# Small products of a mixer set back behind their feeders, and an MLP's turns with another share for GpSimd

## The chip, the cores and the metric

The kernel runs on one core of a Trainium2 chip. The metric is the device time of one execution in microseconds (us), the median over runs. A core has TensorE (PE: matrix products, with a separate weight load, PEld), VectorE (DVE), ScalarE (ACT), GpSimd (POOL) and SyncE (SP, which here issues all DMA transfers). Every engine works through its own instructions in order; they wait for each other through semaphores.

## The reference

Two layers of an encoder on 1024 tokens of 1024 features, all in float32:

```python
for l in range(DEPTH):
    h = rms_norm(x, norm_mix[l])
    z = h @ w_in[l]                       # 2560 columns: q k v | q_h i_h f_fw f_bw g_h | a_c g_c
    o_att = block_attention(q_a, k_a, v_a)            # 8 heads of 64, 2 kv heads, QK norm, axial RoPE
    o_hg  = hgrn2_bidirectional(q_h, i_h, f_fw, f_bw, g_h, ...)   # 4 heads, gated recurrence both ways
    o_cv  = conformer_conv(a_c, g_c, ...)             # gate, depthwise conv of 31 taps, LayerNorm, swish
    x = x + concat([o_att, o_hg, o_cv]) @ w_out[l]
    h = rms_norm(x, norm_mlp[l])
    x = x + jnp.square(jax.nn.relu(h @ w1[l])) @ w2[l]      # 1024 -> 4096 -> 1024
```

## The kernel before

Activations lie with features on the 128 partitions and tokens along the free axis, in tiles of 128 x 1024. A float32 product is made of three passes over parts of reduced precision: `split` (L203) and `parts` (L894) copy a value to a high part on ScalarE and subtract it on VectorE for the low part; then high x high, high x low, low x high go to TensorE. A dense column (`zsteps`, L300, through `dense_steps`, L214) is 48 products of 128 x 512 into one of the two S banks of PSUM; its weights are split by `wtile` (L194), its result is taken out by `evac` (L316, L322) times the norm's factor.

**The mixer.** Twenty columns of z come in the order `ZORDER`: the convolution's four, then those of the first `Hgrn` object (two of the four recurrence heads), v, k, four of q, then those of the second. The convolution is 62 shifted multiply-adds on VectorE (L344, L352) and a LayerNorm (`conv_tail`). The recurrence (`Hgrn.core`) starts with `near`, goes through levels of block length 1 to 64, each with score products (`scores`, L494, taken out by VectorE at L501 or by predicated copies at L505) and updates (L525 on VectorE and GpSimd, L526), then transposes its keys (L539), makes the states (L549, L555, L558) and the outputs (L583, taken out at L587). The parts for v, k and q (`vpart`, `kpart`, `qpart`) square, sum over tokens (`tok_sums`, L162), take a root in a chain of some 11 small VectorE instructions (`rstd`, L151 to L156), rotate (`rope`, L621 to L624) and store. A row of factors is widened by ScalarE (`widen`, L168) and transposed by TensorE (`flip`, L178).

These parts are Python generators. A `yield` marks where another part may put its instructions; `next` on a generator emits them up to the next `yield`. So the place of a `yield` sets which instructions stand between a feeder and its consumer. Before the attention this loop mixes three of them: the q, k and v columns (`qg`), the convolution (`cg`) and the first recurrence:

```python
for _ in h0.core():
    for g in (qg, cg, qg, cg):
        next(g, None)
```

The framework then orders each engine's instructions by priority (the order in which they were written, or higher under `tc.high_priority`) and by when it takes their inputs to be ready. The result is the order shown below.

**Attention** runs 64 units (a head, a half, 128 queries): scores two units ahead (L745), VectorE's scaling with the row's extreme (L756), exponent (ScalarE, L759), division (GpSimd, L761), transposes (L782), values (L803). `gen`, the second recurrence, is taken one step at every second unit. Where it ends, the output projection's inputs for the recurrence and the convolution are split.

**The MLP** uses a seven-product scheme (M1 to M7, as Strassen's and Winograd's) on blocks, once for each of its two matrices. The first matrix goes in 16 pairs of tiles; `product` makes 12 products for one M and takes out the bank (ScalarE at L1022 to L1039; VectorE in `join`, L1004, then the activation at L1008 and L1009, and differences at L1035 and L1042 to L1044). Four M ahead, `w_parts` and `x_parts` make sums and differences (L904, L907) and splits. For the first 14 products (two pairs, taken side by side) the splits follow each other in written order (`ordered`). `row[0]` is the engine of the sums; it becomes GpSimd at product 10, and VectorE again 14 before the end. The results go to DRAM (`ad`) and come back as operands of the second matrix (`load_a`, L1063), into tiles m (14 buffers) or xs. The second matrix goes in 28 turns; `collect` adds banks to the residual (`acc`, L1175), which `load_acc` (L1098) brings from DRAM: four tiles of kind x, four of kind m.

## Time and profile before

| | us |
|---|---|
| median of three runs | 2546.32 |
| lowest, highest | 2542.85, 2547.26 |
| the profiled execution, its span | 2548.54, 2546.8 |
| busy in the span: PE, DVE, ACT, POOL | 2451.1, 2003.2, 1202.9, 779.0 |
| mean granted TensorE clock | 0.988 of full |

A page of the profile gives one execution: busy time by engine, the chain of work that ended last, the groups of instructions by source line. Views of the trace give the same for a window of time. "a<-b" is what an instruction writes and reads, "[2.21 <-DVE tmp L1004]" the idle time of its engine before it and what ended it. Line numbers are those of the kernel before.

### The profile page before, as it was taken

The page shows a single profiled execution, that of the slowest core. Times are in us where ns is not written, and L with a number is a line of the kernel's source. Part 1 is how long each engine was busy: PE and PEld are TensorE (multiplying, and loading weights), DVE is VectorE, ACT ScalarE, POOL GpSimd, SP SyncE. Part 2 cuts the span into 40 slices and gives each one's busy share as a digit, 9 for nine tenths or more (in the row PEclk, how much of TensorE's full clock was granted, in tenths as well). Part 3 has the DMA queues.
Part 4 walks back from the last instruction along what each step waited for, and adds up shares of the span by engine and source line. Part 5 has one row for each costly group of instructions (what it writes and reads, how often), then busy time and mean ns, then how long its engine had stood idle before and what let it go on. Part 6 is the DMA issues. An engine that isn't in the chain of part 4 may idle for free.

```text
span 2546.8 us, 34055 instructions
## 1 busy us (share of the span) xinstructions
PE 2451.1 (96%) x12608; PEld 2020.0 (79%) x12608; DVE 2003.2 (79%) x3023; ACT 1202.9 (47%) x1960; POOL 779.0 (31%) x491
## 2 busy tenths in 40 slices
PE   8989999999999999999999899999999999999999
PEld 7767778878778887888887777888787888878887
DVE  5998598872887777987859985898639877789876
ACT  4222478863544443443423225787635444444332
POOL 0232566433154430000123325664331544200000
PEclk9999999999999999999999999999999999999999
DMA  4101310032244448454221113000322444574442
GB/s 157 60 25 63 103 35 18 14 124 96 83 168 158 148 166 302 162 175 152 69 106 50 42 63 104 18 18 26 133 90 95 163 143 167 191 260 155 162 155 91
DMA packets 113077, 286.99 MB, mean 113 GB/s; under 512 B 11408, under 2 KB 11664, under 8 KB 112912
## 3 DMA queue, kind: packets, MB, share of 16 engines
q1 hardware_dynamic: 112912, 284.83, 32.2%
q8 instruction: 99, 1.62, 0.3%
q14 instruction: 66, 0.54, 0.1%
HBM read 197.75 MB, written 87.03 MB: 112 GB/s over the span
## 4 chain that ended last, share of the span: by engine, by line
PE 77%; DVE 14%; ACT 3%; issue 2%; POOL 2%; DMA 1%; SPq 0%; DVEq 0%; ACTq 0%; POOLq 0%
PE S L223 15%; PE S L1195 10%; PE c L995 9%; PE e L1195 7%; PE c L1195 6%; PE e L995 6%; PE S L995 6%; DVE x L352 4%; PE e L803 4%; PE c L782 3%; PE S L745 3%; PE e L494 2%; PE e L162 1%; PE e L583 1%; DVE P L756 1%
## 5 line engine op out<-in xcount | busy, mean ns | idle before, releaser
L223 PE MATMUL S<-xs,whi 128*128 128x512 f32 x1280 | 363.7, 405 | 10.4 <-ACT xs L208 8.9
L223 PEld LDWEIGHTS S<-xs,whi 128*128 128x128 f32 x1280 | 243.3, 193 | 66.2 <-ACT xs L208 8.9
L223 PE MATMUL S<-xs,wlo 128*128 128x512 f32 x640 | 203.3, 398 | 0.0
L1195 PE MATMUL S<-xs,xs 128*128 128x512 f32 x816 | 201.2, 390 | 0.3 <-DVE xs L897 0.3
L896 ACT ACTIVATE xs<-m 128x512 fp32r<-128x512 f32 x216 | 126.0, 619 | 157.4 <-DVE m L907 52.3
L761 POOL TENSOR_SCALAR P<-P,mx 128x1024 f32<-128x1024 f32 x124 | 142.4, 1149 | 162.8 <-DVE mx L760 125.3
L787 DVE TENSOR_TENSOR PT<-c,PT 128x512 fp32r<-128x512 f32 x256 | 171.1, 684 | 23.0 <-ACT PT L786 21.5
L786 ACT ACTIVATE PT<-c 128x512 fp32r<-128x512 f32 x256 | 147.3, 593 | 67.7 <-PE c L782 64.2
L1195 PEld LDWEIGHTS S<-xs,xs 128*128 128x128 f32 x816 | 153.1, 188 | 32.8 <-DVE xs L897 1.2
L199 ACT ACTIVATE whi<-raw 128x1024 fp32r<-128x1024 f32 x56 | 59.1, 1058 | 245.9 <-PE S L223 232.8
L803 PE MATMUL e<-PT,x 128*128 128x256 f32 x1024 | 172.3, 298 | 0.8 <-ACT PT L786 0.5
L756 DVE TENSOR_SCALAR_CACHE_REDUCE P<-S,nqc 128x1024 f32<-128x1024 f32 x124 | 158.6, 1279 | 13.9 <-PE S L745 8.7
L352 DVE SCALAR_TENSOR_TENSOR x<-x,par,x 128x1009 f32<-128x1009 f32 (+14 forms) x120 | 166.7, 1390 | 1.8
L897 DVE TENSOR_TENSOR xs<-m,xs 128x512 fp32r<-128x512 f32 x216 | 144.9, 694 | 24.8 <-ACT xs L896 24.8
L260 POOL TENSOR_TENSOR tmp<-tmp,tmp 128x1024 f32<-128x1024 f32 x19 | 50.6, 2664 | 364.4 <-ACT tmp L259 364.2
L782 PE MATMUL c<-cons,P 128*128 128x128 f32 x992 | 151.9, 277 | 10.5 <-POOL P L761 5.6
L745 PE MATMUL S<-x,QS 128*128 128x512 f32 x480 | 153.8, 419 | 4.9 <-DVE P L756 4.6
L759 ACT ACTIVATE P<-P,mx 128x1024 f32<-128x1024 f32 x124 | 142.5, 1149 | 24.6 <-DVE P L756 23.3
L1195 PE MATMUL e<-xs,xs 128*128 128x512 f32 x552 | 142.9, 395 | 7.2 <-ACT xs L896 6.8
L803 PEld LDWEIGHTS e<-PT,x 128*128 128x128 f32 x1024 | 138.9, 193 | 8.5 <-ACT PT L786 2.2
L782 PEld LDWEIGHTS c<-cons,P 128*128 128x128 f32 x992 | 115.1, 141 | 36.7 <-issue 10.4
L223 PEld LDWEIGHTS S<-xs,wlo 128*128 128x128 f32 x640 | 122.4, 192 | 26.6 <-issue 0.3
(310 smaller groups left out, 5679.3 us busy)
## 6 DMA issues: line engine op xcount, KB each, us to landing
m<-ad SPq DMA_DIRECT2D x104, 512.0 KB, 3.8
ad<-x SPq DMA_DIRECT2D x176, 256.0 KB, 2.1
raw<-w_in_t SPq DMA_DIRECT2D x40, 512.0 KB, 3.3
xs<-w_t SPq DMA_DIRECT2D x36, 512.0 KB, 3.8
raw<-w_t SPq DMA_DIRECT2D x36, 512.0 KB, 3.6
m<-w_t SPq DMA_DIRECT2D x32, 512.0 KB, 6.3
ad<-tmp SPq DMA_DIRECT2D x48, 256.0 KB, 2.2
x<-w_t SPq DMA_DIRECT2D x24, 512.0 KB, 4.8
```

The costliest lines, as they stand in the source:

```text
L223: nc.tensor.matmul(zp[h] if type(zp) is list else zp[:, h, :], w, xx[:, h * 512 : (h + 1) * 512], start=first, stop=last)
L352: nc.vector.scalar_tensor_tensor(y[:, lo:hi], u[:, lo + d : hi + d], par[:, l, wof + tap : wof + tap + 1], y[:, lo:hi], op0=ALU.mult, op1= ...
L745: nc.tensor.matmul(S[:, hb, :], qs, kk[:, hb * 512 : (hb + 1) * 512], start=first, stop=not first)
L756: nc.vector.tensor_scalar(Pt, S, nqc[:, j, ci : ci + 1], 3.0e38, op0=ALU.mult, op1=ALU.min, accum_out=mx[:, 1:2])
L759: nc.scalar.activation(Pt, Pt, AF.Exp, bias=mx[:, 1:2], scale=-1.0, accum_out=mx[:, 2:3])
L782: nc.tensor.transpose(t[:, q * P : (q + 1) * P], Pt[:, hb, q * P : (q + 1) * P], ident)
L786: nc.scalar.activation(hi, src, AF.Copy)
L787: nc.vector.tensor_tensor(lo, src, hi.bitcast(F32), op=ALU.subtract)
L803: nc.tensor.matmul(pvp[:, cs], VS[g][:, hb * 4 + kb, :], pt[:, kb, :], start=hb == 0 and n == 0, stop=hb == 1 and n == 7,)
L897: ordered("v", nc.vector.tensor_tensor(lo, src, hi.bitcast(F32), op=ALU.subtract))
L995: nc.tensor.matmul(bank, w[i][:, kt * P : (kt + 1) * P], BC[name][kt][j], start=n == 0 and name not in ("M6", "M7", "M3"), stop=n == 11, s ...
L1195: nc.tensor.matmul(banks[dt], w[i][:, dt * P : (dt + 1) * P], a[j], start=n == 0 and name not in ("M6", "M7", "M3"), stop=n == 3 * SG - 1, ...
```

## The change

In the mixer:

- `conv_tail` pauses four and six times between widening and transposing.
- The transposes of the recurrence's v (L442) leave the constructor of `Hgrn` and become `turned`, called from `near` behind two pauses, with one more after each half.
- The key transposes (L539) pause after every half instead of every two.
- `kpart` pauses twice more. The unfinished parts of q, k and v are resumed one step at a time (`resume`), at other steps of the next column, instead of being finished in one go.
- In attention, `gen` takes a step at every unit below 14, then at every second.

In the MLP:

- The bank reads and what follows them in `product` run under high priority for pairs 0 to 2 too, not for the last pair alone.
- `row[0]` becomes GpSimd at product 24 instead of 10; the end of the written order stays at 10.
- The second four residual loads are issued one by one in the second turn, not ahead of the first.

```diff
@@ conv_tail
             w = widen(mc, 1)
+            for _ in range(4):
+                yield
             for h in range(2):
                 b = flip(w, h)
...
             w = widen(rstd(sp[:, 0:8], 8, 1.0), 1)
+            for _ in range(6):
+                yield
@@ Hgrn
                 evac(ztile(8 + ls), iv)
+
+            def turned(self):
                 for h in range(2):
                     tpv = pse()
                     for q in range(4):
                         c = h * 4 + q
-                        nc.tensor.transpose(tpv[:, q * P : (q + 1) * P], iv[:, c * P : (c + 1) * P], ident)
+                        nc.tensor.transpose(tpv[:, q * P : (q + 1) * P], self.iv[:, c * P : (c + 1) * P], ident)
                     nc.scalar.activation(
-                        vt[:, h * 4 : h * 4 + 4, :], tpv.rearrange("p (a b) -> p a b", a=4), AF.Copy
+                        self.vt[:, h * 4 : h * 4 + 4, :], tpv.rearrange("p (a b) -> p a b", a=4), AF.Copy
                     )
+                    yield
@@ near
                 yield
+                yield
+                yield from self.turned()
                 t = tmp()
@@ core
                             Kt[:, d, g * 4 : g * 4 + 4, :], tk.rearrange("p (a b) -> p a b", a=4), AF.Copy
                         )
-                    yield
+                        yield
@@ kpart
             krw = widen(rstd(sp[:, 0:16], 16, 1.0 / 64), 2)
+            yield
             nc.gpsimd.tensor_scalar(kz, kz, pv(l, "kn"), 0.0, op0=ALU.mult, op1=ALU.add)
             rope(kz)
+            yield
@@ qkv
+            def resume(_=None):
+                if rest and next(rest[0], 1) is not None:
+                    rest.pop(0)
+
             for col, part in [(5, vpart), (4, kpart)] + [(j, lambda zp, j=j: qpart(zp, j)) for j in range(4)]:
                 for k, _ in enumerate(zsteps(col, lambda zp: start(part(zp)))):
-                    if k == 2 and rest:
-                        drain(rest.pop(0))
+                    if len(rest) > 1 or k in ((2, 4) if col == 0 else (6,)):
+                        resume()
                     yield
-            drain(rest.pop(0))
+            while rest:
+                resume()
+                yield
@@ attention
-            if gen is not None and u % 2 == 0:
+            if gen is not None and (u % 2 == 0 or u < 14):
@@ product
-            with tc.high_priority() if p == NPAIR - 1 else nullcontext():
+            with tc.high_priority() if p < 3 or p == NPAIR - 1 else nullcontext():
@@ the first matrix
             if k == 14 - AHEAD:
                 chain = None
+            if k == 24:
                 row[0] = nc.gpsimd
@@ the second matrix
-        for dt in R4:
-            load_acc(1, dt)
...
+                if k == 1:
+                    load_acc(1, dt)
```

Three places show how the instructions move. The first is TensorE at the end of the first recurrence in layer 0. L223 is a dense product: S_235 is the last q column, S_278 the column after it, S_295 the second column after the q columns in the new order. L583 (L592 now) are the recurrence's output products. Before:

```order
L549 MATMUL e_1621<-vt_467,T_1492 64x64 x16
L223 MATMUL S_235_1517<-xs_135,whi_1208 128x512 x2
L223 MATMUL S_235_1517<-xs_136,whi_1208 128x512 x2
...
L583 MATMUL e_1660<-A_789,vt_467 64x128 x2
L223 MATMUL S_235_1517<-xs_145,wlo_1209 128x512 x2
L223 MATMUL S_278_1825<-xs_103,whi_1362 128x512 x2
...
L583 MATMUL e_1660<-X_465,m_227_1493 64x128 x2
```

and of the change:

```order
L223 MATMUL S_295_1939<-xs_140,whi_1480 128x512
L162 MATMUL e_1711<-cons_77,tmp_1709 128x1 x8
...
L592 MATMUL e_1725<-A_777,vt_467 64x128 x2
L223 MATMUL S_295_1939<-xs_145,whi_1480 128x512 x2
L223 MATMUL S_295_1939<-xs_146,whi_1480 128x512 x2
L223 MATMUL S_295_1939<-xs_145,wlo_1481 128x512 x2
L592 MATMUL e_1725<-X_465,m_233_1540 64x128 x2
```

The outputs stand more than one dense column further back. Ahead of the third output product there were 737 dense products and are 816.

The second is VectorE in the MLP's opening, layer 0. L897 (L914 now) are splits: m_5841 to m_5850 are the four parts of x for M4, whi_5853 the low part of M4's first weight; L907 (L924) are differences of x; L1004 (L1021) reads a bank, L1008 (L1025) and L1035 (L1052) follow it. Before:

```order
L907 TENSOR_TENSOR x_965_5577<-x_965_5577 128x512
L897 TENSOR_TENSOR m_5841<-x_948_5343,m_5841 128x512
L897 TENSOR_TENSOR m_5844<-x_954_5406,m_5844 128x512
L897 TENSOR_TENSOR m_5847<-x_960_5469,m_5847 128x512
L897 TENSOR_TENSOR m_5850<-x_965_5577,m_5850 128x512
L897 TENSOR_TENSOR whi_5853<-raw_5580,whi_5853 128x512
L1004 TENSOR_TENSOR x_1028_5869<-S_1027_5856,tmp_5707 128x512
```

and of the change:

```order
L924 TENSOR_TENSOR x_965_5577<-x_965_5577 128x512
L1021 TENSOR_TENSOR tmp_5818<-c_5656,tmp_5669 128x512
L914 TENSOR_TENSOR m_5841<-x_948_5343,m_5841 128x512
L1025 SCALAR_TENSOR_TENSOR tmp_5818<-tmp_5818,Rb_5753 128x512
L1021 TENSOR_TENSOR x_1028_5869<-S_1027_5856,tmp_5707 128x512
L914 TENSOR_TENSOR m_5844<-x_954_5406,m_5844 128x512
L1025 SCALAR_TENSOR_TENSOR x_1028_5869<-x_1028_5869,Rb_5753 128x512
L1021 TENSOR_TENSOR x_1028_5869<-c_5694,tmp_5707 128x512
L1052 TENSOR_TENSOR x_1036_5921<-tmp_5818 128x512
L1025 SCALAR_TENSOR_TENSOR x_1028_5869<-x_1028_5869,Rb_5753 128x512
L914 TENSOR_TENSOR m_5847<-x_960_5469,m_5847 128x512
L914 TENSOR_TENSOR m_5850<-x_965_5577,m_5850 128x512
```

Bank reads and their followers now stand among the splits; one more (L1052) follows, and then whi_5853.

The third is SyncE's queue where the second matrix begins, layer 0. L1098 (L1115 now) loads residuals (xmd), L1063 (L1080) operands (ad), L910 (L927) stores results. Before:

```order
L1098 DMA m_8171<-xmd_74 128x1024
L1098 DMA m_8173<-xmd_74 128x1024
L910 DMA ad_75<-x_1294_8046 128x512 x2
L910 DMA ad_75<-x_1305_8107 128x512
L910 DMA ad_75<-x_1306_8108 128x512 x2
L1098 DMA m_8175<-xmd_74 128x1024
L1098 DMA m_8177<-xmd_74 128x1024
L1063 DMA m_8181<-ad_75 128x2x512
L1063 DMA m_8183<-ad_75 128x2x512
```

and of the change:

```order
L1080 DMA m_8173<-ad_75 128x2x512
L1080 DMA m_8175<-ad_75 128x2x512
L927 DMA ad_75<-x_1294_8046 128x512 x2
L927 DMA ad_75<-x_1305_8107 128x512
L927 DMA ad_75<-x_1306_8108 128x512 x2
L1080 DMA m_8213<-ad_75 128x2x512
L1080 DMA m_8215<-ad_75 128x2x512
L1115 DMA m_8301<-xmd_74 128x1024
```

The operands of the third and fourth turns have the queue places of the residuals, whose first load stands behind them.

## The prediction

> **What bounds the kernel now.** The page's head and the chain of waits came first: who sets the end.
>
> ```profile
> span 2546.8 us, 34055 instructions
> ...
> PE 77%; DVE 14%; ACT 3%; issue 2%; POOL 2%; DMA 1%; SPq 0%; DVEq 0%; ACTq 0%; POOLq 0%
> ```
>
> TensorE work makes 77% of the chain, so it can only shorten where TensorE stands still or runs slowly. Where that is, the busy time by stage tells (columns: stretch, its length, then busy time of PE, PEld, DVE, ACT, POOL with counts, granted clock, DMA share, GB/s).
>
> ```profile
> 70.00:310.00 240.00, 218.60 (x1240) 176.78 (x1239) 205.22 (x287) 75.58 (x92) 79.14 (x34) 0.96 0.16 55
> 310.00:573.00 263.00, 251.20 (x1744) 211.36 (x1743) 219.45 (x408) 198.12 (x341) 144.50 (x114) 0.99 0.17 54
> ...
> 650.00:730.00 80.00, 74.05 (x331) 59.40 (x330) 71.90 (x105) 43.56 (x77) 27.68 (x17) 1.00 0.35 125
> 730.00:960.00 230.00, 230.00 (x1016) 190.58 (x1016) 171.34 (x212) 103.24 (x184) 95.51 (x63) 1.00 0.46 161
> 960.00:1010.00 50.00, 46.67 (x195) 36.94 (x194) 40.71 (x66) 18.72 (x35) 0.00 (x0) 0.97 0.90 324
> ...
> 2225.00:2275.00 50.00, 45.74 (x190) 36.15 (x190) 40.48 (x66) 18.33 (x34) 0.00 (x0) 0.97 0.87 323
> ```
>
> Layer 0 has four places with idle TensorE: the projections with the first recurrence (21.4 us of 240), attention with the second recurrence (11.8), the MLP's opening (6.0), the start of its second product (3.3). Layer 1 repeats them. The body of the MLP is full: 230.00 of 230. So the change is worth something at these four places only. In the first, the waits of TensorE are these (who waited for whom; total, times, longest):
>
> ```profile
> PE e L637 <- DVE A L501: 6.2, 1, 6.2
> PE e L442 <- DVE m L322: 4.3, 1, 4.3
> PE c L539 <- ACT T L540: 3.0, 1, 3.0
> PE e L178 <- ACT tmp L168: 3.0, 2, 1.7
> PE e L162 <- DVE A L505: 2.3, 1, 2.3
> ```
>
> Every one is a small product that stands right behind its feeder, and mostly the feeder is on VectorE. The question is whether VectorE is late because of the order or because it is full. Finer windows of that place, and one of the attention stage:
>
> ```profile
> 110.00:250.00 140.00, 120.73 (x784) 95.75 (x782) 130.24 (x190) 36.45 (x52) 44.99 (x21) 0.94 0.13 46
> 250.00:310.00 60.00, 57.87 (x283) 47.88 (x283) 35.47 (x68) 26.51 (x28) 26.92 (x11) 0.97 0.22 77
> ...
> 200.40:207.10 6.70, 6.70 (x35) 5.79 (x34) 4.96 (x14) 2.56 (x4) 0.22 (x1) 0.50 0.31 109
> 330.00:380.00 50.00, 46.54 (x310) 39.42 (x308) 46.33 (x85) 40.47 (x73) 33.64 (x26) 1.00 0.08 22
> ```
>
> From 110 to 250 us VectorE is busy 130.24 of 140, so it sets the pace there; after that TensorE does (57.87 of 60) and VectorE has 24.5 us to spare. This decides how I price the mixer: waits taken off TensorE in the first stretch count only as far as dense products then left for the second stretch become fewer.
>
> **The first place: dense products pulled ahead of the recurrence's end.** All the new pauses in the convolution's tail, the key part, the recurrence and the resuming of the q, k and v parts do one thing together: TensorE gets dense work between a feeder and its consumer. The listed orders give the amount. Ahead of the third of the recurrence's output products (L583) stand 737 dense products (L223) before and 816 now, that is 79 more, and 16 more of the sums over tokens (L162). Their price:
>
> ```profile
> 241.77 6.82 PE e L583 x84
> ...
> 573.24 76.91 PE S L223 x338
> ...
> L223 PE MATMUL S<-xs,whi 128*128 128x512 f32 x116 | 33.0, 403 | 0.0
> L223 PE MATMUL S<-xs,wlo 128*128 128x512 f32 x59 | 18.9, 401 | 0.0
> ...
> L162 PE MATMUL e<-cons,tmp 128*128 128x2 f32 x32 | 4.2, 262 | 0.0
> ```
>
> The first two rows are of the chain of waits in order of time (start, length, what): 338 dense products in one unbroken piece take 76.91 us, 0.228 each. The next rows are the groups from 242 to 303 us (busy, mean ns), from the recurrence's output to the first attention score: 175 dense products remain there, and 96 will. So 79 x 0.228 = 18.0 us, and 16 x 4.2/32 = 2.1, together 20.1 us of TensorE work leave the stretch where TensorE is the bound.
>
> It is not free. These columns bring VectorE work with them, ahead of its own part of the recurrence's end (L587). The two orders show 3 more convolution taps (L352), 2 weight splits (L200), one evacuation (L322), one rotation (L621, L623, L624), and one more root chain (3 of L154 and 11 others as small). Busy time and mean of one, VectorE, 110 to 250 us:
>
> ```profile
> L352 DVE SCALAR_TENSOR_TENSOR x<-x,par,x 128x1016 f32<-128x1016 f32 (+14 forms) x36 | 48.6, 1349 | 0.3
> L200 DVE TENSOR_TENSOR wlo<-raw,whi 128x1024 fp32r<-128x1024 f32 x7 | 10.8, 1539 | 0.0
> L623 DVE TENSOR_TENSOR tmp<-tmp,x 128x1024 f32<-128x1024 f32 x4 | 8.0, 1999 | 0.0
> L624 DVE TENSOR_TENSOR tmp<-tmp,tmp 128x1024 f32<-128x1024 f32 x4 | 5.7, 1432 | 0.0
> L621 DVE STREAM_SHUFFLE tmp<-tmp 128x1024 f32<-128x1024 f32 x4 | 5.3, 1336 | 0.0
> L154 DVE SCALAR_TENSOR_TENSOR nwt<-nwy 128x16 f32<-128x16 f32 x12 | 4.2, 349 | 0.0
> L322 DVE TENSOR_TENSOR tmp<-S,Rb 128x1024 f32<-128x1024 f32 x2 | 2.4, 1214 | 0.0
> L155 DVE TENSOR_TENSOR nwt<-nwt,nwa 128x16 f32<-128x16 f32 x12 | 2.0, 168 | 0.0
> ```
>
> 3 x 1.35 + 2 x 1.54 + 1.21 + (1.34 + 2.00 + 1.43) + 3 x 0.35 + 11 x 0.168 = 16.0 us. If they fill all of VectorE's idle time in that stretch (140 - 130.24 = 9.8), the recurrence ends 6.2 us later; if none, 16.0. So the first score comes 20.1 - 16.0 = 4.1 to 20.1 - 6.2 = 13.9 us sooner. I take **8 us a layer**, a little under the middle, since some small products will find new waits. The half-speed clock counts for nothing extra in this sum, because VectorE holds that stretch anyway: from 200.4 to 207.1 the clock was 0.50 while TensorE was never idle.
>
> [...]
>
> **Attention.** Taking one step of the second recurrence at every unit up to the fourteenth, for a generator that has grown from 29 to 34 steps, brings some of it forward: at the eighteenth unit the new order has 6 more of the predicated copies (L505), 3 updates (L525) and one product of decays (L526) on VectorE, ten operations of about half a tile, 7 us at 0.69 each (the least of L1042 below) or a little more, and 28 more score products (L494) on TensorE, 3.7 us at 0.13 (L162's 4.2/32). From 330 to 380 us VectorE has 3.7 us idle. So TensorE may wait up to 4 us more there, and is up to 4 us further on with the recurrence, which later units no longer carry. The transposes of v (L442), which wait for VectorE here too, are cut in two and set back. Net **-1 us a layer**, between -3 and +4.
>
> **The MLP's opening.** Two edits. The evacuations of the first three pairs now rank above the splits; and for two more pairs 8 sums and differences of weights, and 6 differences of outputs, 14 in all, go to VectorE instead of GpSimd.
>
> ```profile
> 678.19 2.50 DVE L897 TENSOR_TENSOR m<-x,m 128x512 fp32r<-128x512 f32 x4
> ...
> 681.34 3.02 PE L995 MATMUL S<-m,whi 128*128 128x512 f32 x12 [0.59 <-DVE whi L897]
> ...
> 695.80 3.00 PE L995 MATMUL c<-xs,whi 128*128 128x512 f32 x12 [2.21 <-DVE tmp L1004]
> ...
> 705.12 3.01 PE L995 MATMUL e<-m,wlo 128*128 128x512 f32 x12 [0.87 <-ACT tmp L1027]
> ...
> 714.95 1.42 PE L995 MATMUL c<-m,whi 128*128 128x512 f32 x5 [1.08 <-DVE tmp L1004]
> ...
> L1042 DVE TENSOR_TENSOR x<-tmp,x x16: 689/1789/1794, 698.0 to 2215.8; 128x512 f32<-128x512 f32 x16
> ```
>
> The move costs VectorE nothing: a half-tile difference takes it 0.689 us alone and 1.789 beside a GpSimd operation (least and median of L1042), so each GpSimd operation already costs it up to 1.1. The waits of 2.21, 0.87 and 1.08 are for evacuations, and the priority takes them away: -4.2. Against it stands the order shown ahead: the split that M4's product waits for (whi_5853) now has 12 rows before it behind the four differences, where 4 stood. Eight rows at 0.60 (2.50 for four) make it 4.8 us later, and the product waited for it by 0.59 even before. So a new wait of about 5 us at 681 replaces three later ones. Net **0**, between -4 (both gains, M4 starting on its first tiles) and +6.5 (the wait, and half clock behind it).
>
> **The start of the second product.** The four residual loads (L1098) leave the place ahead of the operands of its third turn.
>
> ```profile
> 968.21 1.07 SPq L1098 DMA_DIRECT2D m<-xmd  x2
> ...
> 982.03 12.06 SPq L1063 DMA_DIRECT2D m<-ad  x7
> ...
> 989.77 0.51 PE L1195 MATMUL e<-xs,xs 128*128 128x512 f32 x1 [2.29 <-ACT xs L896]
> ...
> 992.34 0.79 PE L1195 MATMUL e<-xs,xs 128*128 128x512 f32 x1 [0.64 <-ACT xs L896]
> ```
>
> SyncE's queue gave the first two free m tiles, at 968.21, to residuals, and the turn's own operands went out from 982.03; TensorE stood 2.29 + 0.64 us for them. The operands now take the queue places of 968.21, 13.8 us sooner, which is more than the wait. With 2.9 us of waits and the clock's 3% of 50 us (1.5), **-4 us** in layer 0 and **-3.5** in layer 1, whose stage has 4.3 us idle in all; between -1.5 and -5. What is late next: the four residuals, now issued among the operands of the following turns. They are first read when the third turn ends, and the bank is needed again only after another turn, 48 x 0.228 = 10.9 us on, so a late one is covered.
>
> **The sum**: 2 x (-8 - 1 + 0) - 4 - 3.5 = -25.5 us. The profiled execution took 2548.5 us (span 2546.8 and 1.7 around it): 2523. It lies 2.2 above the median of the three runs, 2546.3, so I expect **2521 us**.
>
> **Rivals.** (1) The waits at the first place go altogether, because VectorE's order, not its load, was at fault: then the 21.4 us idle and 4% of 240 us of slow clock (9.6) go, 23 us a layer more than I count: 2475. For it: every wait there is a feeder just ahead. Against: 130.24 of 140.
> (2) The waits only change their names: the recurrence ends the full 16 us later, new waits eat the 4.1 us left, and the operands' loads meet the next tile that is not free, so that 1 us a layer remains: 2544.
> (3) Slower: VectorE's extra 16 us at the first place are stretched by GpSimd, whose updates and rotation products run beside them. The place is 110 to 250 us; L1042 shows a factor of 2.6 in the worst case. From a factor of 25/16 = 1.6 on (20.1 us pulled ahead, and 5 saved elsewhere) the change loses; at a factor of 2 it loses 7 us a layer: 2560. Against it: the means used above already hold the overlap of that stretch.
>
> **How the numbers follow.** Forecast 0.66, from 2505 to 2540: the first place at its ends gives 2509 to 2529, and the MLP's opening moves that by -8 to +13 for two layers; (1) 0.10; (2) 0.12; (3) 0.12. A measurement of this kernel tells about 0.2%, 5 us, from no change. Faster: the forecast, (1) and the lower edge of (2), 0.78. Within: most of (2), 0.10. Slower: (3), 0.12. The range reaches halfway to (1) and takes in (2): 2496 to 2546.
>
> **What would show it.** In the waits of 70 to 310 us, those for L442, L637 and L539 should shrink below 1 us each, and VectorE should stay above 93% until the recurrence's output products, which should begin 6 to 16 us later than at 241.8; the first score should come 4 to 14 us sooner. In the MLP's opening one wait of 3 to 6 us for a split should stand where four small ones stood. The waits at 989 and 992 should be gone and residual loads should land unwaited for. I am wrong if the first score comes no sooner, if attention takes over 4 us longer, or if M4's wait exceeds 7 us.

## The result and the profile after

| | before | after |
|---|---|---|
| median, us | 2545.22 (6 runs) | 2560.34 (6 runs) |
| lowest, highest | 2542.85, 2548.22 | 2559.80, 2564.66 |
| ratio, 95% interval | | 1.0058 [1.0047, 1.0069] |
| span of the profiled execution | 2546.8 | 2558.4 |

The change makes the kernel 0.6% slower. 2521 was forecast; 2560 lies outside the range, on the side to which 0.12 was given. The page of the changed kernel has this head, these busy times and this chain by engine:

```profile
span 2558.4 us, 34038 instructions
...
PE 2470.6 (97%) x12608; PEld 2029.9 (79%) x12608; DVE 1983.8 (78%) x3051; ACT 1208.2 (47%) x1964; POOL 715.0 (28%) x463
...
PE 35%; DVE 2%; ACT 1%; POOL 1%; issue 0%; DVEq 0%; POOLq 0%
```

The shares of the chain come to 39% only, where those of the kernel before came to nearly all: it was followed back over less than half of the span, and says nothing of the rest. So the stretches carry the reading. The same six stretches as in the prediction, now of the changed kernel (length, busy PE, PEld, DVE, ACT, POOL, granted clock, DMA share, GB/s):

```profile
70.00:310.00 240.00, 223.00 (x1229) 176.97 (x1228) 203.15 (x287) 71.98 (x89) 66.92 (x31) 0.94 0.16 53
310.00:573.00 263.00, 246.42 (x1696) 207.62 (x1694) 214.57 (x406) 199.38 (x341) 145.42 (x116) 0.97 0.15 50
650.00:730.00 80.00, 76.29 (x329) 60.77 (x328) 69.41 (x114) 42.15 (x72) 4.08 (x2) 0.96 0.30 109
730.00:960.00 230.00, 230.00 (x1016) 190.44 (x1015) 171.51 (x214) 103.21 (x182) 98.32 (x65) 1.00 0.44 153
960.00:1010.00 50.00, 49.80 (x218) 40.18 (x217) 40.29 (x66) 21.22 (x40) 0.00 (x0) 1.00 0.93 343
2225.00:2275.00 50.00, 50.00 (x222) 41.22 (x221) 37.80 (x62) 20.63 (x37) 0.00 (x0) 1.00 0.92 334
```

Two columns have to be read together: what PE lacks of the length, and what the clock lacks of 1. In the first place TensorE now idles 17.0 us rather than 21.4, but the slow clock takes 6% of 240 us, 14.4, rather than 9.6: the one has eaten the other. Attention idles 16.6 rather than 11.8, and the clock takes 7.9 rather than 2.6: some 10 us lost. The MLP's opening has 2.2 us less idle and 3.2 us more of slow clock. The start of the second product is clean in both layers.

The events of the timeline give the same by stage. "Up to scores" runs from the layer's start (layer 1: from the last product of layer 0) to the first attention score, "attention" on to the MLP's first product, then the two matrices. In each cell stand layer 0 and layer 1, in us:

| kernel | up to scores | attention | first matrix | second matrix |
|---|---|---|---|---|
| before | 302.0, 290.5 | 348.0, 349.4 | 315.3, 314.9 | 310.9, 315.8 |
| after | 304.2, 288.8 | 357.6, 357.9 | 315.9, 316.0 | 307.1, 311.0 |

Of the 11.6 us between the two spans, attention has lost 18.1, the second matrix has won 8.6, and the first place and the opening come to +2.1 in sum. Work can move from "up to scores" into attention, so that a gain in the one may be a loss in the other; run 10 below is such a case. And one execution gives a stage only within some 3 us: layer 0 up to the first score took 300.5 to 303.1 us in the kernel before and the runs 3 to 6, which have the same mixer.

### The profile page after: what moved, and what is told of

The parts are those of the page before. It is cut to its first block, busy times and chain, and to the rows that moved or that the text cites. A ratio compares the mean times of both kernels' runs of the same rounds, so it can differ in the third digit from the quotient of the medians.

```text
span 2558.4 us, 34038 instructions
## 1 busy us (share of the span) xinstructions
PE 2470.6 (97%) x12608; PEld 2029.9 (79%) x12608; DVE 1983.8 (78%) x3051; ACT 1208.2 (47%) x1964; POOL 715.0 (28%) x463
## 5 line engine op out<-in xcount | busy, mean ns | idle before, releaser
L223 PE MATMUL S<-xs,whi 128*128 128x512 f32 x1280 | 366.9, 407 | 11.6 <-ACT xs L208 8.9
L223 PEld LDWEIGHTS S<-xs,whi 128*128 128x128 f32 x1280 | 243.0, 194 | 68.8 <-ACT xs L208 8.9
L223 PE MATMUL S<-xs,wlo 128*128 128x512 f32 x640 | 203.1, 399 | 0.0
L913 ACT ACTIVATE xs<-m 128x512 fp32r<-128x512 f32 x216 | 126.0, 619 | 141.6 <-DVE m L924 50.7
L803 ACT ACTIVATE PT<-c 128x512 fp32r<-128x512 f32 x256 | 148.1, 594 | 92.2 <-PE c L799 90.2
L804 DVE TENSOR_TENSOR PT<-c,PT 128x512 fp32r<-128x512 f32 x256 | 170.5, 684 | 16.6 <-ACT PT L803 15.7
L352 DVE SCALAR_TENSOR_TENSOR x<-x,par,x 128x1009 f32<-128x1009 f32 (+14 forms) x120 | 173.3, 1444 | 1.6
L914 DVE TENSOR_TENSOR xs<-m,xs 128x512 fp32r<-128x512 f32 x216 | 145.0, 695 | 22.0 <-ACT xs L913 22.0
L223 PEld LDWEIGHTS S<-xs,wlo 128*128 128x128 f32 x640 | 123.5, 194 | 26.1
L799 PEld LDWEIGHTS c<-cons,P 128*128 128x128 f32 x992 | 115.3, 141 | 34.7 <-issue 11.8
```

The source lines that it names most:

```text
L223: nc.tensor.matmul(zp[h] if type(zp) is list else zp[:, h, :], w, xx[:, h * 512 : (h + 1) * 512], start=first, stop=last)
L352: nc.vector.scalar_tensor_tensor(y[:, lo:hi], u[:, lo + d : hi + d], par[:, l, wof + tap : wof + tap + 1], y[:, lo:hi], op0=ALU.mult, op1= ...
L799: nc.tensor.transpose(t[:, q * P : (q + 1) * P], Pt[:, hb, q * P : (q + 1) * P], ident)
L803: nc.scalar.activation(hi, src, AF.Copy)
L804: nc.vector.tensor_tensor(lo, src, hi.bitcast(F32), op=ALU.subtract)
L914: ordered("v", nc.vector.tensor_tensor(lo, src, hi.bitcast(F32), op=ALU.subtract))
```

## The experiments

Each was timed beside the kernel before on the same chip; the ratio is to that kernel. The stages of all of them stand in a table at the end of this section, and behind it a table of attention in three stretches.

**1. The tail's pauses and the keys.** In the changed kernel TensorE stands 6.8 us at the start of attention. The rows of SyncE's queue, of TensorE and of ScalarE around it (start, length, engine, what; in brackets the idle time before and what ended it):

```profile
312.79 0.45 SPq L730 DMA_DIRECT2D tmp<-kd  x1
318.95 2.68 SPq L404 DMA_DIRECT2D mixd<-tmp  x2
321.68 0.45 SPq L731 DMA_DIRECT2D tmp<-kd  x1
322.24 2.62 SPq L746 DMA_DIRECT2D tmp<-qd  x4
...
325.88 1.06 ACT L205 ACTIVATE x<-tmp 128x1024 fp32r<-128x1024 f32 x1 [4.03 <-DMA tmp<-kd]
...
329.91 1.06 ACT L803 ACTIVATE PT<-c 128x512 fp32r<-128x512 f32 x2
...
330.54 0.58 PE L820 MATMUL e<-PT,x 128*128 128x256 f32 x1 [6.79 <-ACT PT L803]
```

The same queue in the kernel before:

```profile
304.10 5.04 SPq L400 DMA_DIRECT2D mixd<-tmp  x2
309.65 0.45 SPq L713 DMA_DIRECT2D tmp<-kd  x1
310.16 0.58 SPq L714 DMA_DIRECT2D tmp<-kd  x1
```

The ten pauses have pushed the tail's two stores (L404) behind the first key load. In these rows the queue goes in order: the stores, which wait for the tail's last results, go out at 318.95 us, the second half of the keys behind them at 321.68, 8.9 behind the first; ScalarE's split of the keys (L205, 325.88) stands behind that, and behind the split, on ScalarE, the copies of the transposed probabilities (L803, 329.91), for which TensorE's product waits 6.79 us. So the changed kernel without the pauses:

```diff
@@ conv_tail @@
-            for _ in range(4):
-                yield
...
-            for _ in range(6):
-                yield
```

> The changed kernel without the ten pauses in the convolution's tail; everything else as changed. Theory K (keys behind the tail): the pauses make the tail end so late that its two stores stand between the two halves of the second key load in SyncE's queue (first half out at 312.8, second at 321.7), ScalarE's key split waits for it, and the exponents queued behind that split leave TensorE idle for 6.8 us and at half clock for 6.8 more. Without the pauses the stores stand well ahead of the key loads: the 6.8 us wait at L820 goes in both layers, 8 to 11 us a layer, 2560 -> 2541 (2537 to 2545). Theory S (steps): attention is slow because the second recurrence takes a step at every unit up to the fourteenth; then the wait stays and the time stays at 2556 to 2562.

Measured 2553.74 (2550.35 to 2556.93), ratio 1.0025 [1.0016, 1.0034]. The time lies between the two ranges. The wait of 6.8 us (6.5 in layer 1) is gone in both layers, and 2.7 and 7.0 us of attention with it. So the wait was of the kind named, but taking it away is worth 6.6 us in all, not the 15 and more that it was given. The trace shows what ate the rest: from 310 to 573 us TensorE idles 17.7 us, 16.6 in the changed kernel, as its waits for VectorE grew (5.5 us for 1.9 at the scaled scores, 3.7 for 2.5 at the transposed probabilities). What went is slow clock: 0.99 of full for 0.97.

**2. Late steps of the second recurrence.** Before, its generator made a step at every second unit of attention and ended at unit 58; the change steps at every unit up to the fourteenth, and with five steps more ends at unit 54. Here the extra steps stand at the end:

```diff
-            if gen is not None and (u % 2 == 0 or u < 14):
+            if gen is not None and (u % 2 == 0 or u > 48):
```

> The changed kernel, but the second recurrence's generator takes a step at every second unit up to 48 and then at every one, so that it ends at unit 58 as before, not at 54. Theory K with its second part, Q (the last query behind the recurrence's store): in the changed kernel the last query load stands behind the store of the recurrence's result in SyncE's queue, so its split ends late (TensorE idle 3.1 us at 554 and half clock for 3.4); with the late end that load stands ahead again, 3 to 5 us a layer come off, and the 6.8 us wait near 324 stays: 2551 (2547 to 2555). Theory S: the early units lose their extra VectorE work, the 9 us by which the ninth unit of the changed kernel lies behind go: 2542 (2538 to 2546).

Measured 2557.53 (2555.51 to 2560.63), ratio 1.0041 [1.0029, 1.0054]; above both ranges, with attention at 357.5 and 356.9, as in the changed kernel. I took this to acquit the early steps. That was wrong, as the runs 13, 15 and 16 show: the end was later, but the extra steps were bunched again, only elsewhere.

**3 and 4. The MLP's edits alone, and the residual loads alone**, both on the kernel before, with its mixer.

```diff
@@ 3: all three edits of the MLP; 4: the last two hunks alone @@
-            with tc.high_priority() if p == NPAIR - 1 else nullcontext():
+            with tc.high_priority() if p < 3 or p == NPAIR - 1 else nullcontext():
...
+            if k == 24:
                 row[0] = nc.gpsimd
...
-        for dt in R4:
-            load_acc(1, dt)
...
+                if k == 1:
+                    load_acc(1, dt)
```

> The kernel before with the three MLP edits alone, the mixer untouched. By the stage times of the two traces: the second matrix 4.3 us a layer shorter, the opening 0.8 longer, so 7 us under before: 2538 (2535 to 2541). If the second matrix gained only because the mixer shifted something, no difference: 2544 to 2547.

> The kernel before with the later residual loads alone. The prediction's own term: 4 and 3.5 us, 7.5 in all, and by the stage times 8.6: 2537 (2535 to 2539). Against the run with all three MLP edits this gives the price of the priority and of the move from GpSimd to VectorE together: 1 to 2 us if the stage times hold, nothing or a gain if the prediction's middle holds.

Measured 2543.02 (2541.42 to 2545.25), ratio 0.9986 [0.9978, 0.9995], 2 us over what was expected, and 2538.57 (2535.79 to 2539.32), ratio 0.9965 [0.9953, 0.9978], as expected. The loads give 8.3 us. The other two MLP edits together cost 4.4, and the mixer's edits 17.3 (2560.3 - 2543.0).

**5 and 6. Ranking and share apart**, each beside the moved loads (the first, and the second hunk of the diff above).

> The kernel before with the residual loads moved and the evacuations of the first three pairs ranked above the splits; the GpSimd share is as before. The loads alone took 2538.6 us, all three edits of the MLP 2543.0, so that 4.4 us (2.2 a layer) belong to the ranking or to the share. Theory P (the ranking): the one split that a product of the opening waits for stands behind more evacuations on its engine; 2542 to 2545, with a wait of 2 us or more at a product of the first pairs. Theory G (the share): 2536 to 2540.

> The kernel before with the residual loads moved and GpSimd's share of the MLP's sums beginning at the product of number 24; no new ranking. Theory P (the ranking costs the 4.4 us): 2536 to 2540, as the loads alone. Theory G (14 more operations on VectorE in the opening cost it): 2542 to 2545, with waits of TensorE for VectorE in the opening, or VectorE over 95% busy there.

Measured 2548.67 (2544.99 to 2552.46), ratio 1.0007 [0.9999, 1.0016], for the ranking, and 2533.32 (2532.65 to 2535.80), ratio 0.9948 [0.9937, 0.9960], for the share. The ranking costs 10.1 us over the loads alone, more than either theory had; the share gains 5.2, which neither theory had either. In the first matrix it is +3.7 and +3.8 against -5.0 and -5.0. Of these 10.0 us of the share, 4.4 are lost again in the other stages of its trace, 2.1 of them up to the first score of layer 0, where the two kernels do not differ yet. The rows for the share, 690 to 710 us, first of the loads alone, then with the share:

```profile
690.00:710.00 20.00, 18.18 (x73) 14.56 (x73) 19.34 (x21) 8.42 (x15) 12.87 (x9) 0.91 0.48 172
```

```profile
690.00:710.00 20.00, 20.00 (x90) 16.57 (x89) 19.74 (x34) 10.88 (x19) 0.00 (x0) 1.00 0.62 222
```

VectorE gets through 34 operations in 19.74 us alone, and through 21 in 19.34 beside nine of GpSimd. They are not all of one kind, but TensorE's side is plain: 90 products for 73. The rows for the ranking, waits of TensorE from 650 to 780 us in the run with all three edits, and its window 670 to 690:

```profile
PE c L995 <- ACT wlo L896: 3.3, 2, 3.0
PE c L995 <- DVE whi L897: 0.6, 1, 0.6
...
670.00:690.00 20.00, 15.91 (x58) 11.09 (x57) 19.90 (x34) 13.09 (x25) 0.00 (x0) 0.90 0.29 106
```

The window with loads and share, without the ranking:

```profile
670.00:690.00 20.00, 18.26 (x80) 14.15 (x80) 19.77 (x33) 13.93 (x27) 0.00 (x0) 1.00 0.34 114
```

ScalarE makes half of the weights' splits as well as evacuations. The changed kernel's ScalarE and TensorE at that wait:

```profile
693.38 0.61 ACT L1026 ACTIVATE tmp<-tmp 128x512 f32<-128x512 f32 x1
693.89 0.57 ACT L1046 ACTIVATE tmp<-e 128x512 f32<-128x512 f32 x1
694.37 1.14 ACT L913 ACTIVATE xs<-x 128x512 fp32r<-128x512 f32 x2
695.41 0.62 ACT L1026 ACTIVATE x<-x 128x512 f32<-128x512 f32 x1
695.93 0.62 ACT L913 ACTIVATE wlo<-raw 128x512 fp32r<-128x512 f32 x1
...
696.60 0.53 PE L1012 MATMUL c<-m,wlo 128*128 128x512 f32 x1 [2.99 <-ACT wlo L913]
```

Three operations of the evacuation (L1026, L1046) stand within 2.6 us ahead of the one split (L913, 695.93) that the product needs, and 6.8 us of half clock follow. That this queue is the ranking's cost is read from the trace; what the runs show is the cost of the ranking as a whole.

**7. The q, k and v parts resumed piece by piece**, with the two pauses in the key part, beside the moved loads.

```diff
@@ qkv @@
                 for k, _ in enumerate(zsteps(col, lambda zp: start(part(zp)))):
-                    if k == 2 and rest:
-                        drain(rest.pop(0))
+                    if len(rest) > 1 or k in ((2, 4) if col == 0 else (6,)):
+                        resume()
                     yield
-            drain(rest.pop(0))
+            while rest:
+                resume()
+                yield
```

> The kernel before with the residual loads moved, the q, k and v parts resumed piece by piece and the two pauses in the key part. Of the mixer's 17 us (2560.3 with all edits, 2543.0 with those of the MLP alone) the tail's pauses explain some 6.6 and the early steps 2.8; about 8 are open. Theory R (resuming these parts spreads VectorE's work over more of TensorE's, so that the recurrence ends later and keys and queries come later): 2543 to 2548, with the first score over 2 us later than at 300.5 us. Theory T (the v transposes set back, behind two pauses, open a new chain of waits in the recurrence): 2534 to 2540 for this kernel, and waits for L637 gone.

Measured 2530.28 (2527.92 to 2540.40), ratio 0.9945 [0.9930, 0.9961]. The resuming gains 8.3 us over the loads alone by the medians, 5.1 by the ratios. That is below both ranges, though the intervals of the two ratios overlap a little ([0.9930, 0.9961] and [0.9953, 0.9978]). The wait of 5.7 us for L637 is gone; up to the first score it is 1.6 and 8.1 us less. Of the mixer's edits this is the one that gains.

**8, 10 and 11. The v transposes set back.** In the changed kernel's first place a new wait of 5.8 us stands highest:

```profile
PE e L480 <- DVE tmp L473: 5.8, 1, 5.8
PE e L178 <- ACT tmp L168: 4.0, 2, 2.4
PE e L162 <- POOL tmp L368: 2.6, 1, 2.6
PE e L471 <- ACT vt L449: 1.9, 1, 1.9
...
PE e L448 <- DVE m L322: 0.4, 1, 0.4
```

The waits for L442 (now L448), L637 and L539 went, as forecast; these came. The theory was that the transposes now take both small banks between the recurrence's own products. Run 8 sets them back, alone beside the loads; run 11 puts in only the pauses that come with them; run 10 takes both out of the changed kernel.

```diff
@@ 8: near, with the transposes moved into turned(), halved by a pause @@
                 yield
+                yield
+                yield from self.turned()
@@ 11: near, transposes left where they were @@
                 yield
+                yield
+                yield
+                yield
@@ 8 and 11 @@
-            if gen is not None and u % 2 == 0:
+            if gen is not None and (u % 2 == 0 or u < 6):
@@ 10: the changed kernel, near @@
                 yield
-                yield
-                yield from self.turned()
```

> The kernel before with the residual loads moved and the v transposes set back behind two pauses and halved, with three extra steps in the first units of attention so that the later steps of the second recurrence fall to the same units as before. Theory T: transposes that take both banks between the recurrence's own products make the next product wait for an evacuation that is queued behind VectorE and ScalarE; 2543 to 2548, a wait of 4 us or more in 110 to 150 us for TensorE with half clock behind it. Theory R (the resuming costs the 8 us): 2535 to 2540.

> The kernel before with the residual loads moved, and the three pauses that the set-back transposes bring into the recurrence's first part, while the transposes stay where they were; three extra steps in the first units of attention as in the run with the transposes set back. Theory Pl (the place of the transposes: they take both small banks between the recurrence's own products, and the next of these waits for an evacuation): 2536 to 2545, no wait of 5 us at the second pair of those products. Theory Pa (the pauses: three more steps of dense work ahead of the recurrence delay its end on VectorE by 15 us or more): 2555 to 2565.

> The changed kernel with the v transposes back in their old place, without the pauses that came with them; all other edits stay. Alone, on the kernel before, that edit took 24.5 us (2538.6 to 2563.1), all of it before the first score (315.0 and 299.9 us, where 300.5 and 290.5 stood). Theory T (it is the cause in the changed kernel too, where the resuming hid most of it): 2538 to 2547, the first score of layer 0 at 288 to 295 us, attention still 355 us or more, since the tail's pauses and the early steps stay. Rival (pauses can hide each other, so that the rest of the edits has its own loss): 2552 to 2560.

Measured 2563.07 (2560.68 to 2566.82), ratio 1.0064 [1.0052, 1.0076], for run 8; 2568.71 (2564.63 to 2577.85), ratio 1.0073 [1.0059, 1.0087], for run 11; 2585.09 (2583.87 to 2585.71), ratio 1.0143 [1.0129, 1.0157], for run 10; all three are slower than any of their theories had. The wait of the set-back transposes is there in run 8:

```profile
PE e L476 <- DVE tmp L469: 5.8, 1, 5.8
```

In run 11 it is not (its row has 2.0 at the same product), and that kernel is no faster. So the theory of the banks falls: a wait of 5.8 us, the longest of its stretch, was not what the edit costs. The three pauses cost it: with them alone the recurrence's output products begin at 254.5 us, where 235.4 stood, and the first score comes 14.9 and 12.7 us later. (The trace of run 11 is of its slowest execution, 9.1 us over the median.)

In the changed kernel the same edit gains 25 us. Without it, in run 10, the first score comes 16.0 and 13.1 us sooner, but attention takes 26.2 and 28.4 us longer, and that loss stands at attention's start: 99.1 us to the score of unit 14, where the changed kernel takes 63.9. The convolution takes two steps with each step of the first recurrence; with three steps fewer its tail, which has the ten pauses, ran on into attention. TensorE waits there for the tail's row of factors (L168) and its squares (L387), and the second key load (L726) stands behind the tail's stores (L404), 23 us behind the first:

```profile
317.54 0.45 SPq L725 DMA_DIRECT2D tmp<-kd  x1
337.69 3.07 SPq L404 DMA_DIRECT2D mixd<-tmp  x2
340.80 0.45 SPq L726 DMA_DIRECT2D tmp<-kd  x1
...
PE e L178 <- ACT tmp L168: 7.8, 1, 7.8
...
PE e L162 <- POOL tmp L387: 4.4, 1, 4.4
```

So it is the first experiment's mechanism once more, and stronger. The same pauses were a loss in one surrounding and a gain in the other, where with them the tail's stores went out 14.8 us behind the first score rather than 49.5. That run 10 also ends the second recurrence sooner, at unit 48 rather than 54, does not show as a loss: from the score of unit 44 on it takes 177.4 us, the changed kernel 182.6.

**9 and 12 to 15. What adds up, and what doesn't.** Run 9 has three parts on the kernel before: the loads, the share, the resuming. Run 12 adds the early steps and the pause between the halves of the turned keys; 13 the early steps alone; 14 that pause alone, with two extra steps that keep the end at unit 58; 15 as many extra steps as 13, but in the middle.

```diff
@@ 12 and 13 @@
-            if gen is not None and u % 2 == 0:
+            if gen is not None and (u % 2 == 0 or u < 14):
@@ 12 and 14: core, after the copy of the turned keys @@
-                    yield
+                        yield
@@ 14 @@
-            if gen is not None and u % 2 == 0:
+            if gen is not None and (u % 2 == 0 or u in (19, 39)):
@@ 15 @@
-            if gen is not None and u % 2 == 0:
+            if gen is not None and (u % 2 == 0 or 28 < u < 42):
```

> The kernel before with three parts of the change: the residual loads moved, GpSimd's share beginning at the product of number 24, and the q, k and v parts resumed piece by piece with the key part's two pauses. One by one against the loads alone (ratio 0.9965) the share gave 0.9948 and the resuming 0.9945. Theory A (they act in different stages, so they add): ratio 0.992 to 0.994, 2526 to 2532 us, layer 0's stages near 299, 348, 310 and 307 us. Rival: what the resuming brings forward in the mixer is lost in attention when the MLP's share changes where the next layer begins; 0.9945 or above.

> The three parts together, and besides them the pause between the halves of the turned keys (K) and the step of the second recurrence at every unit up to the fourteenth; so all of the change but the tail's pauses, the set-back transposes and the ranking in the MLP. Theory E (the early steps crowd VectorE in the first units of attention): 4 to 9 us over the three parts, with attention at 351 us or more in both layers. Rival (attention's loss in the changed kernel came from the tail's pauses and the set-back transposes alone): within 3 us of the three parts, attention 347 to 350 us.

> The three parts with the step of the second recurrence at every unit up to the fourteenth, without the pause between the halves of the turned keys. With both, attention took 369.3 and 369.1 us for 349.6 and 348.7. Theory End (the early steps: the recurrence's steps fill TensorE's pauses in attention, and with 7 extra ones they run out at unit 44 rather than 58): 2545 to 2558. Theory Kp (the pause between the halves, which holds a small bank over a step): 2522 to 2530.

> The three parts with the pause between the halves of the turned keys, and two extra steps of the second recurrence, one at unit 19 and one at 39, so that it ends at unit 58 as before. Theory End: within 4 us of the three parts (2521 to 2529). Theory Kp: 2545 or more.

> The three parts with seven extra steps of the second recurrence at the odd units 29 to 41 instead of the first fourteen; it ends at unit 44 in both. Theory End (what counts is when the steps run out): as the early steps, 2545 to 2558, lost in the units after 44. Theory Crowd (steps at every unit put small products right behind their feeders in units that are full of the mixer's tail): within 8 us of the three parts, 2522 to 2533, the first 14 units as fast as in the three parts (first score to the fifteenth unit 63 us, where both edits took 80).

| run | median (lowest to highest) | ratio, interval |
|---|---|---|
| 9, three parts | 2525.08 (2518.87 to 2529.39) | 0.9907 [0.9891, 0.9924] |
| 12, and early steps and keys' pause | 2556.81 (2553.43 to 2560.12) | 1.0033 [1.0021, 1.0044] |
| 13, and early steps | 2552.56 (2544.85 to 2561.23) | 1.0021 [1.0010, 1.0032] |
| 14, and keys' pause | 2531.04 (2523.89 to 2536.37) | 0.9935 [0.9923, 0.9947] |
| 15, and steps in the middle | 2539.90 (2535.37 to 2543.31) | 0.9969 [0.9957, 0.9981] |

The three parts add, a little better than forecast, and are faster than both kernels. Of the 32 us that run 12 loses on them, where 4 to 9 were forecast, the early steps have 27.5; the pause alone costs 6.0, 2 more than forecast for it, and a small part. Run 15 falls between its two theories, 14.8 us over the three parts, and the same seven steps at the start, in run 13, cost 12.7 more. Two things can be read. Crowding: from the first score to that of unit 14 run 13 takes 80.3 us, run 15 63.4 and run 9 62.8. The clock of that place, run 9 and then run 13:

```profile
315.00:365.00 50.00, 44.92 (x280) 36.90 (x279) 45.98 (x80) 36.55 (x65) 32.67 (x24) 0.97 0.17 50
```

```profile
315.00:380.00 65.00, 59.27 (x321) 47.85 (x320) 53.09 (x90) 39.39 (x69) 35.47 (x27) 0.84 0.10 29
```

TensorE is as busy as before (0.91 of the stretch for 0.90), at 0.84 of the clock, and no wait there is longer than 2.6 us. My reading is that these are small products, each a little behind its feeder, that never fill it; no run tests that alone. The early end: the queue of SyncE in run 13, and TensorE's wait from 479 to 579 us.

```profile
503.45 12.94 SPq L856 DMA_DIRECT2D tmp<-mixd  x2
516.48 0.38 SPq L601 DMA_DIRECT2D mixd<-tmp  x1
517.32 4.73 SPq L856 DMA_DIRECT2D tmp<-mixd  x2
522.10 8.67 SPq L737 DMA_DIRECT2D tmp<-qd  x6
...
PE S L753 <- POOL QS L743: 5.2, 2, 3.7
```

The kernel before, the same queue:

```profile
484.34 25.12 SPq L729 DMA_DIRECT2D tmp<-qd  x4
...
552.21 0.32 SPq L601 DMA_DIRECT2D mixd<-tmp  x1
```

The recurrence's store (L601) and the loads of the mixer's outputs around it (L856) now stand ahead of six query loads (L737); in the kernel before the last query load (L729) was out 42 us ahead of the store. In run 15 the order is the same, with six query loads from 514.64 us on. From the score of unit 44 on TensorE idles 9.6 us in run 13 and 12.2 in run 15, and 5.4 in run 9. But that the early end costs the same 14.8 us in both is not shown: run 13 takes 5.0 us less than run 9 there, because work has moved ahead of it, and its whole loss stands before unit 44, 17.5 us of it in the first 14 units. Run 15 loses 8.0 behind unit 44 and 1.3 before.

**16 to 18. The changed kernel without the suspects, and the other direction.** Run 16 is the changed kernel without the tail's pauses and with the five extra steps spread, so that the recurrence ends at unit 58 again; run 18 has no ranking either; run 17 is the three parts of run 9 with a recurrence that starts at unit 2 and ends at 60.

```diff
@@ 16 and 18, beside the edit of run 1 @@
-            if gen is not None and (u % 2 == 0 or u < 14):
+            if gen is not None and (u % 2 == 0 or u % 12 == 1 and u < 50):
@@ 18 @@
-            with tc.high_priority() if p < 3 or p == NPAIR - 1 else nullcontext():
+            with tc.high_priority() if p == NPAIR - 1 else nullcontext():
@@ 17 @@
-            if gen is not None and u % 2 == 0:
+            if gen is not None and u % 2 == 0 and u >= 2:
```

> The changed kernel without the tail's pauses, and with the second recurrence's extra steps at units 1, 13, 25, 37 and 49, so that it ends at unit 58 as before, not at 54. Without the tail's pauses alone it was 2553.7 us, with 354.9 and 350.9 us of attention. Theory End or Crowd: attention back to 347 to 351 us in both layers, 2546 to 2551. Rival (attention's rest comes from the set-back transposes and halved keys themselves): 2552 to 2557.

> The changed kernel without the three suspects: no pauses in the tail, the extra steps spread over the units, no new ranking in the MLP. With the ranking it was 2542.1. The ranking cost 6.3 and 6.3 us of the first matrix's stage where the share is moved (316.3 and 316.3 us against 310.0 and 310.0); so 2528 to 2533, the first matrix 309 to 311 us in both layers. Rival (the ranking costs less where the mixer hands over otherwise): 2536 or more.

> The three parts with the second recurrence's steps beginning at unit 2, not 0, so that it ends at unit 60, not 58. If what counts is only when the steps run out, the later end gains: 2519 to 2525 (the three parts: 2525.1). If the recurrence's end must also leave room for its store and the splits behind it, it loses: 2526 to 2533, in the units from 58 on.

Measured 2542.07 (2539.10 to 2546.75), ratio 0.9982 [0.9973, 0.9990], for run 16; 2529.55 (2528.38 to 2534.84), ratio 0.9938 [0.9925, 0.9952], for run 18; 2515.02 (2511.33 to 2518.72), ratio 0.9877 [0.9864, 0.9891], for run 17. Run 16 has the attention that was expected or a little less, and in all comes out 4 us below its range; run 18 is inside its range, run 17 4 us below its lower theory. The row of run 16 for the stretch that the changed kernel lost:

```profile
310.00:573.00 263.00, 251.17 (x1752) 212.01 (x1751) 219.13 (x413) 199.68 (x345) 142.20 (x113) 0.99 0.14 45
```

So the changed kernel's loss is closed by three removals: the tail's pauses 6.6 us, the bunched steps with their end at unit 54 11.7, the ranking 12.5, in that order, 30.8 in all; what is left of the change is 0.6% faster than the kernel before. Run 16 spreads the steps and moves their end at once, so it does not tell the two apart. And run 18 keeps the set-back transposes with their pauses: it takes 7.4 and 7.0 us more up to the first score than the three parts, and 4.5 us more in all. Run 17, with a later start and a later end, takes 10.1 us less than the three parts by the medians, 7.6 by the ratios: it is the fastest kernel of all here, 1.2% below the kernel before. In the stretch of attention TensorE is the busiest of all these kernels:

```profile
310.00:573.00 263.00, 252.93 (x1753) 214.83 (x1753) 219.10 (x409) 199.08 (x342) 141.65 (x115) 0.99 0.17 54
```

Whether it is the later start or the later end that gains, no run tells apart: TensorE idles 2.4 us less than in run 9 between the scores of units 14 and 44, 2.6 less behind them, and 1.5 more ahead.

The stages of the runs, as in the table above:

| run | up to scores | attention | first matrix | second matrix |
|---|---|---|---|---|
| 1 no tail pause | 305.2, 291.6 | 354.9, 350.9 | 316.3, 316.3 | 307.6, 311.3 |
| 2 late steps | 301.6, 288.8 | 357.5, 356.9 | 316.3, 314.9 | 307.6, 311.3 |
| 3 MLP only | 300.5, 289.4 | 349.6, 350.7 | 316.3, 316.1 | 306.9, 310.9 |
| 4 loads only | 300.5, 290.5 | 349.3, 347.9 | 315.0, 315.0 | 307.4, 311.0 |
| 5 loads, ranking | 303.1, 290.6 | 350.8, 349.7 | 318.7, 318.8 | 307.6, 310.9 |
| 6 loads, share | 302.6, 291.5 | 348.0, 349.5 | 310.0, 310.0 | 307.2, 312.2 |
| 7 loads, resuming | 298.9, 282.4 | 348.6, 349.6 | 314.9, 314.9 | 307.8, 310.9 |
| 8 loads, transposes | 315.0, 299.9 | 348.3, 347.6 | 315.0, 315.0 | 306.8, 311.3 |
| 9 three parts | 300.4, 284.8 | 349.6, 348.7 | 310.0, 310.0 | 307.0, 312.1 |
| 10 after, unturned | 288.2, 275.7 | 383.8, 386.3 | 316.2, 315.3 | 307.1, 311.2 |
| 11 loads, pauses | 315.4, 303.2 | 354.3, 354.2 | 315.0, 315.4 | 307.5, 310.9 |
| 12 five parts | 296.8, 280.6 | 369.3, 369.1 | 310.0, 310.0 | 307.0, 311.2 |
| 13 early steps | 297.2, 283.7 | 365.3, 365.8 | 310.0, 310.0 | 307.1, 311.6 |
| 14 keys' pause | 298.0, 280.6 | 358.4, 358.1 | 310.0, 310.0 | 308.6, 310.9 |
| 15 middle steps | 297.0, 287.0 | 358.9, 359.5 | 310.0, 310.0 | 307.0, 312.0 |
| 16 spread steps | 308.0, 294.6 | 346.8, 345.8 | 315.5, 315.4 | 307.2, 310.9 |
| 17 later end | 300.9, 286.9 | 345.6, 344.7 | 309.9, 310.0 | 307.9, 311.1 |
| 18 no ranking | 307.8, 291.8 | 345.8, 346.9 | 310.0, 309.9 | 307.5, 311.5 |

Attention of layer 0 in three stretches, bounded by the first score, the score of unit 14, that of unit 44 and the MLP's first product (each unit has four score products, so that their count gives the bounds). In each cell stand the length and TensorE's idle time in it, in us; the lengths of layer 1 lie within 4 us of these:

| kernel | to unit 14 | to unit 44 | to the MLP |
|---|---|---|---|
| before | 61.5, 5.6 | 114.0, 3.0 | 172.5, 3.9 |
| after | 63.9, 8.6 | 111.1, 1.2 | 182.6, 8.5 |
| 1 no tail pause | 61.1, 5.4 | 110.3, 2.5 | 183.4, 10.2 |
| 16 spread steps | 52.8, 3.8 | 119.9, 2.9 | 174.1, 6.3 |
| 10 after, unturned | 99.1, 23.0 | 107.3, 2.0 | 177.4, 9.4 |
| 9 three parts | 62.8, 5.5 | 114.1, 3.0 | 172.7, 5.4 |
| 13 early steps | 80.3, 8.0 | 117.3, 2.6 | 167.7, 9.6 |
| 15 middle steps | 63.4, 5.2 | 114.8, 2.7 | 180.7, 12.2 |
| 17 later end | 62.0, 7.0 | 111.1, 0.6 | 172.5, 2.8 |

The changed kernel loses 2.4 us to the score of unit 14, wins 2.9 to that of unit 44, and loses 10.1 behind it.

## Why the prediction was wrong

**The first place: wrong.** Forecast -8 us a layer, found +2.2 and -1.7. The step that failed is the premise that VectorE sets the pace there, so that all the new pauses "do one thing together" and dense work moved ahead is only an exchange, 20.1 us of TensorE against 6.2 to 16.0 of VectorE. Three windows of the changed kernel:

```profile
110.00:250.00 140.00, 129.34 (x750) 102.43 (x749) 129.26 (x184) 36.80 (x53) 44.49 (x23) 0.94 0.13 48
...
110.00:271.00 161.00, 147.77 (x856) 115.77 (x854) 142.07 (x212) 38.91 (x55) 46.83 (x24) 0.92 0.14 48
262.00:304.00 42.00, 39.52 (x243) 29.85 (x242) 19.69 (x41) 16.18 (x17) 7.74 (x4) 0.94 0.28 88
```

VectorE was to stay above 93% until the recurrence's output; it was 92% busy over 140 us and idled 18.9 us over 161. The output products came not 6 to 16 us later than at 241.8 (the third of them) but at 266.4, 24.6 later. What the runs show in its place is that the pauses are not alike: the three ahead of the recurrence's levels, with no other edit but the loads, set the output products back by 19.1 us and the first score by 14.9 and 12.7 (run 11), while the resuming alone brings the first score 1.6 and 8.1 us forward (run 7). So a busy share of 93% did not mean that VectorE set the pace. That the recurrence is a chain through TensorE, ScalarE and VectorE, in which each pause lets a step of dense work pass, is my reading of it. The 16 sums over tokens that were counted as pulled ahead are 32 in the traces (112 for 80), 2.1 us more at the price used. That TensorE idled less (by 4.4 us) and lost more to the slow clock (by 4.8) was left out, with the words that the clock "counts for nothing extra in this sum, because VectorE holds that stretch anyway". Rival (2), that waits only change their names, comes nearest to what happened at this place, though the recurrence ended later than its 16 us.

**Attention: wrong, and the largest part.** Forecast -1 a layer, between -3 and +4; found +9.6 and +8.5. The sum counted operations against idle time in 50 us of the stretch and left out SyncE's queue. The step that failed is the one that took the steps brought forward as work "which later units no longer carry": up to unit 44 that came out near (+2.4 and -2.9 us in layer 0), but behind it, where the sum had nothing, the changed kernel takes 10.1 us longer, with a query load behind the recurrence's store (547.68 and 546.77 us) and a wait of 3.1 us for it. With the tail's pauses out and the steps spread up to unit 58 (run 16) 8.5 of the 10.1 go, and attention is 1.2 us shorter than before. The tail's pauses did not enter this term at all, although they set the tail's stores between the two key loads; and the extra steps were priced by their busy time (7 us, with 3.7 free), not by what they do to the clock and to the order of the last query loads. The prediction's list of signs had "if attention takes over 4 us longer".

**The MLP's opening: the sum near by luck, both terms wrong.** Forecast 0; found +0.6 and +1.1 in the changed kernel. The ranking was to take 4.2 us of waits away and to bring one of about 5 us; it cost 3.7 alone and 6.3 with the share moved. The share was priced at nothing; it gained 5.0 us a layer in the first matrix. The two errors cancel. One wait of 3.0 us for a split stands there, as forecast (3 to 6), but on ScalarE, behind ranked evacuations, not on VectorE behind the four differences. The half clock behind the wait, part of the forecast's upper edge, came too: 6.8 us at 0.50. The estimate that the move costs VectorE nothing, since a half-tile difference takes 0.689 us alone and 1.789 beside GpSimd, was right as far as it went and should have been carried on to a gain.

**The start of the second product: right.** Forecast -4 and -3.5; found -3.8 and -4.8, and 8.3 us with the loads alone. From 960 to 1010 us TensorE waits only 0.2 us, and that for a split: no residual load is waited for.

**The rivals.** Rival (3) gave 2560, and 2560 was measured, but that is a coincidence: GpSimd was to stretch VectorE's work between 110 and 250 us, and there GpSimd was busy 44.49 us, 44.99 before, and VectorE 129.26, 130.24 before. Rival (1), that all waits of the first place go, is refuted by the new ones, though the resuming alone has shown that part of it was there to take. (Halfway from 2521 to it is 2498, not the 2496 of the range; nothing hangs on it.)

## What to carry to other kernels

Where one engine issues all transfers, as SyncE here, a pause put into one stream moves that stream's stores past another stream's loads; read that queue's order on both sides of an edit before pricing anything else, since a store waits for the last result of its stream and here the key load behind it went out late too (8.9 us behind the first in the changed kernel, 23 in run 10). A generator that feeds another loop is filler with a rate: spread its steps over the whole loop, for steps that were bunched and ended four units sooner cost 12 us here, and try a later start and end, which gained 8 to 10. A pause's worth depends on where it stands: three of them cost 30 us in one kernel, and with the transposes between them saved 25 in another. Before ranking an evacuation first, ask which product waits for what else its engine does; the longest wait of a stretch need not be its cost (5.8 us that went in run 11 without gain).
